# Hybrid attention block on one core: the first stage takes raw x, the norm's weight goes into the weights and its token scale into the results

## The chip, the core and the metric

The kernel runs on one core of a Trainium2 chip. The metric is the device time of one execution in microseconds (us). An execution is also profiled: its span runs from the first to the last instruction. The engines are TensorE (PE; its weight loads, PEld, stand apart), VectorE (DVE), ScalarE (ACT), GpSimd (POOL) and SyncE (SP), which issues most of the DMAs. TensorE's clock has two levels, 1.2 and 2.4 GHz, and the profile tells which was granted.

## What is computed

One decoder block over 512 tokens of width 1024, in float32. Cut to what the change touches:

```python
h = rmsnorm(x, norm_mix)          # x * rsqrt(mean(x*x) + EPS) * norm_mix
P = h @ w_in                      # q, k, v of mixer A; q, k, v (three branches) and gates of mixer B; merge gates
y_A = sliding_window_attention(...) @ w_up_a
y_B = native_sparse_attention(...) @ w_up_b
x = x + (sigmoid(g_a) * y_A + sigmoid(g_b) * y_B) @ w_out
x = x + conv_ffn(rmsnorm(x, norm_ffn))
out = rmsnorm(x, norm_final)
```

With r(t) the scale of token t, h[t, d] = x[t, d] * r(t) * norm_mix[d]. So h @ W equals r(t) times x @ (norm_mix[d] * W).

## The kernel before

A product is made of three matmuls on rounded parts (type fp32r): an operand is split into a high part (a copy that rounds) and a low part (the operand less its high part), and `three` (L104) adds high x high, high x low and low x high in PSUM. `split` (L87) makes the parts: ACT copies the high part, VectorE subtracts for the low part (L94), or GpSimd does so in pieces of 256 columns for the names in `POOLJ`.

The first stage is written out by hand. `FIRST` (L33) is a list of steps, and `do` (L178) emits each; the order of the list is the order on each engine, since engines run their queues in order. x has four tiles of 128 tokens (`t`), and the width two halves of four blocks (`h`, `k`). The steps:
- `dum`: filler matmuls on a tile of ones (L170).
- `gh`, `gl`, `ga`: high and low part of the norm weight as one row, and a matmul with ones that spreads it over the partitions (L189).
- `sq`, `ms`, `r`: squares of a tile on ACT with their sum (L195), mean on VectorE (L198, L199), power -1/2 on GpSimd (L201).
- `sc`: x times scale times norm weight, on VectorE in place (L204).
- `tp`, `xh`, `xl`: four transposes (L209), the high part `xTh` (ACT, L215) and the low part `xTl` (VectorE, L217).
- `wh`, `wl`: parts of the value weight `wv` (1024 x 408: the value columns and the branch gates), two blocks of 408 columns at a time (ACT L219, GpSimd L221).
- `v`: value matmuls (L228), 24 for each tile; a step's digits are tile, half, which of the three products, block pair.
- `va`, `la`, `vb`, `lb`, `eg`, `g`: parts of the values and the branch gates out of PSUM (L231 to L245).
- `pg`, `pgc`: the bias table spread by a one-hot matmul (L247 copies the table, L250, L253).

After it come jobs in the order `AORD` (L23): projections `ka`, `qa0`, `qa1`, `kc`, `qa2` and so on. `proj_job` (L287) loads a weight block of 1024 columns (`weight`, L96, DMA on SP), splits it, and runs 24 matmuls into a PSUM bank; its `evac` then copies the result into its slot, for `ka` `keys` (L404, ACT L413 and L414, VectorE L415 and L416), for queries `queries` (L419). PSUM has eight banks; projections use the two of tag `mm` in turn (`BANKS`, L42). `filler` (L300) feeds jobs to TensorE between the steps of the attention units; outside the first stage a planner with a simulated timeline orders the instructions. `need` (L324) asks for `ka`, `qa0` and `qa1` ahead of the first attention unit. `toeplitz` (L514) loads the bias table, stored to DRAM before, with shifted rows, into the slot that a value weight part leaves; the scores add it (L540).

Of the kernel before, what the change touches and what calls it, by code (L numbers as in the profile page):

```python
# [11 lines left out]
P = 128  # L12
# [46 lines left out]
def hybrid(tc, x, wv, wblk, w1, w2, wua, wub, wout, wfi, wfo, nmix, nffn, nfin, sinks, par, table, onehot, out):  # L59
# [9 lines left out]
    with es:  # L69
# [51 lines left out]
        wvr = [slot(7 + h, [P, 4, NV], F32, f"wvr{h}") for h in range(2)]  # L121
# [37 lines left out]
        junk = WR.tile([P, D], F32, tag="raw", name="junk", bufs=RAW)  # L159
        first = FIRST.split()  # L160
        st, ps_v, tp_x, out_v = {}, {}, {}, {}
        pgs = ((0, ZA, 0), (ZA, ZA + 512, 1), (ZA + 512, ZA + ZW, 1))

        def wv_of(w, h, c):
            return w[h][:, 2 * c : 2 * c + 2]

        def busy(n):

            for i in range(n):
                T.matmul(bank("mm", "idle"), one[:, :P], one, start=True, stop=True)  # L170
# [6 lines left out]

        def do(u):  # L178
            n = [int(c) for c in u if c.isdigit()]
            what = u.rstrip("0123456789")  # L180
            if what == "dum":
                busy((7, 2, 3, 3)[n[0] - 1])
            elif what == "gh":
                V.tensor_copy(gr[:, 0, halves[n[0]]], grow[:, halves[n[0]]])
            elif what == "gl":
                V.tensor_tensor(gr[:, 1, halves[n[0]]], grow[:, halves[n[0]]], f(gr[:, 0, halves[n[0]]]), op=ALU.subtract)
            elif what == "ga":
                for i in range(2):
                    T.matmul(gam[n[0]], one[:1, :P], gr[:, i, halves[n[0]]], start=(i == 0), stop=(i == 1))  # L189
            elif what in ("sq", "sqa", "sqb"):  # L190
                t = n[0]
                if t not in st:
                    st[t] = [SM.tile([P, c], F32, tag=g, bufs=3, name=f"{g}x_{t}") for g, c in (("s2", 2), ("ssq", 1), ("rstd", 1))]
                for i in {"sq": (0, 1), "sqa": (0,), "sqb": (1,)}[what]:
                    A.activation(junk[:, halves[i]], xt[t][:, halves[i]], AF.Square, accum_out=st[t][0][:, i : i + 1])  # L195
            elif what == "ms":
                s2, m, _ = st[n[0]]
                V.tensor_scalar(m, s2[:, 0:1], 1.0 / D, EPS, op0=ALU.mult, op1=ALU.add)  # L198
                V.tensor_scalar(m, s2[:, 1:2], 1.0 / D, m, op0=ALU.mult, op1=ALU.add)  # L199
            elif what == "r":  # L200
                G.tensor_tensor(st[n[0]][2], st[n[0]][1], mhalf, op=ALU.pow)  # L201
            elif what == "sc":
                t, h = n
                V.scalar_tensor_tensor(xt[t][:, halves[h]], xt[t][:, halves[h]], st[t][2], gam[h], op0=ALU.mult, op1=ALU.mult)  # L204
# [5 lines left out]
            elif what in ("xh", "xl"):  # L210
                t, h = n
                pv = tp_x[t, h].rearrange("p (k q) -> p k q", k=4)
                hi, lo = xTh[h][:, :, t * P : (t + 1) * P], xTl[h][:, :, t * P : (t + 1) * P]
                if what == "xh":
                    xlast[0] = A.copy(hi, pv)  # L215
                else:
                    xlast[1] = V.tensor_tensor(lo, pv, f(hi), op=ALU.subtract)  # L217
            elif what == "wh":
                A.copy(wv_of(wvh, *n), wv_of(wvr, *n))  # L219
            elif what == "wl":  # L220
                G.tensor_tensor(wv_of(wvl, *n), wv_of(wvr, *n), f(wv_of(wvh, *n)), op=ALU.subtract)  # L221
            elif what == "v":
                t, h, i, c = n
                if t not in ps_v:
                    ps_v[t] = bank(("mm", "mm", "o", "mm")[t], f"v{t}")
                mine = [w for w in first if w[0] == "v" and w[1] == str(t)]
                for k in range(4 * h + 2 * c, 4 * h + 2 * c + 2):
                    T.matmul(ps_v[t][:, :NV], (xh, xh, xl)[i](k)[:, t * P : (t + 1) * P], (wvh, wvl, wvh)[i][h][:, k % 4],  # L228
                             start=(u == mine[0] and k % 2 == 0), stop=(u == mine[-1] and k % 2 == 1))
            elif what == "va":  # L230
                A.copy(VA[:, n[0], :, 0:64], out_of(n[0])[0])  # L231
            elif what == "la":
                V.tensor_tensor(VA[:, n[0], :, 64:128], out_of(n[0])[0], f(VA[:, n[0], :, 0:64]), op=ALU.subtract)
            elif what == "vb":
                A.copy(VB[:, n[0], :, 0:64], out_of(n[0])[1])
            elif what == "lb":
                V.tensor_tensor(VB[:, n[0], :, 64:128], out_of(n[0])[1], f(VB[:, n[0], :, 0:64]), op=ALU.subtract)
            elif what == "eg":
                A.activation(out_of(n[0])[2], ps_v[n[0]][:, 384:408], AF.Exp, scale=-1.0)
            elif what == "g":  # L240
                t, eg = n[0], out_of(n[0])[2]
# [4 lines left out]
            elif what == "pg":
                V.tensor_copy(tabc, tab.rearrange("p (b h) -> p b h", b=2)[:, :, None].to_broadcast([33, 2, 16, 8]))  # L247
                for i, (c0, c1, b) in enumerate(pgs):
                    pgs_t.append(bank("pt", f"pg{c0}"))
                    T.matmul(pgs_t[i][:, : c1 - c0], tabc[:, b].rearrange("p c h -> p (c h)"), oh[:, c0:c1], start=True, stop=True)  # L250
            elif what == "pgc":
                for i, (c0, c1, b) in enumerate(pgs):
                    A.copy(gsb[:, c0:c1], pgs_t[i][:, : c1 - c0])  # L253
            else:
# [4 lines left out]
        with tc.manual_schedule():
# [5 lines left out]
            nc.scalar.dma_start(grow, nmix)  # L265
            A.activation(warm[:, 0:1], warm[:, 0:1], AF.Exp)
            for h in range(2):
                nc.sync.dma_start(xt[0][:, halves[h]], x[0:P, halves[h]])
            for h in range(2):
                for c in range(2):  # L270
                    nc.sync.dma_start(wv_of(wvr, h, c), wv[h][:, 2 * c : 2 * c + 2])
                if h == 0:
                    nc.sync.dma_start(xt[1], x[P : 2 * P])
            for t in range(2, NT):
                nc.sync.dma_start(xt[t], x[t * P : (t + 1) * P])
            nc.sync.dma_start(tab[:32], table)
            nc.sync.dma_start(oh, onehot)
            nc.sync.dma_start(prm, par)
            nc.sync.dma_start(nsink, bc(sinks, 8))
            gam = [bank("sc", f"gam{h}") for h in range(2)]  # L280
# [19 lines left out]
        def filler():  # L300
            with tc.issue_after(xlast[0].ins), tc.issue_after(xlast[1].ins):
# [158 lines left out]
        for nm in AORD.split():  # L460
# [503 lines left out]
```

## Time and profile before

| | us |
|---|---|
| median of 3 runs | 763.36 |
| lowest, highest | 761.96, 763.41 |
| profiled execution, device time | 764.42 |
| its span, first to last instruction | 762.6 |

The profiled execution is one more run of the kernel; times read from its trace are counted from the start of its span. "Busy" of TensorE counts pipelined matmuls, so that it can be near 100% at half clock too.

### The profile page before, as it was taken

How to read it: one execution, taken by the hardware profiler on the slowest of the kernel's cores; microseconds unless marked ns; L12 is line 12 of the kernel's file. 1: busy time of each engine (PE TensorE's matmuls, PEld its weight loads, DVE VectorE, ACT ScalarE, POOL GpSimd, SP SyncE). 2: the span in 40 equal slices, each digit the busy share in tenths (PEclk: the TensorE clock that was granted, in tenths of full speed). 3: DMA queues.
4: the chain of work that ended last, by engine and by line, in shares of the span. 5: the costliest groups of instructions: out<-in, count | busy, mean ns of one | idle time of the engine just before them, and what ended most of it. 6: DMA issues, size and time to landing. Idle time of an engine off the chain costs nothing.

```text
span 762.6 us, 9931 instructions
## 1 busy us (share of the span) xinstructions
PE 744.4 (98%) x3602; PEld 623.1 (82%) x3602; DVE 427.6 (56%) x902; ACT 368.2 (48%) x686; POOL 183.5 (24%) x258
## 2 busy tenths in 40 slices
PE   8999999999999999999999999999999999999996
PEld 6887787788888888878889888888888888888885
DVE  6627787456655568757365656565656564214223
ACT  6435777556656765664335444444344433113213
POOL 5234747434433545405400000000000000002001
PEclk9999999999999999999999999999999999999998
DMA  8363239312111121405322232323232324332302
GB/s 301 110 147 98 92 91 246 101 66 83 46 68 56 58 81 35 159 4 191 111 83 83 83 111 83 110 84 111 83 111 84 110 83 138 91 103 89 105 28 110
DMA packets 25582, 76.74 MB, mean 101 GB/s; under 512 B 3868, under 2 KB 6044, under 8 KB 25534
## 3 DMA queue, kind: packets, MB, share of 16 engines
q1 hardware_dynamic: 25532, 76.12, 31.3%
q8 instruction: 28, 0.46, 0.3%
q14 instruction: 20, 0.16, 0.1%
q10 hardware_dynamic: 2, 0.00, 0.0%
HBM read 72.96 MB, written 3.15 MB: 100 GB/s over the span
## 4 chain that ended last, share of the span: by engine, by line
PE 87%; DVE 5%; ACT 3%; DMA 2%; issue 2%; POOL 0%; SPq 0%; POOLq 0%; DVEq 0%; ACTq 0%
PE ug L105 11%; PE ug L106 11%; PE ug L107 10%; PE fo L857 5%; PE fo L859 5%; PE fo L858 5%; PE pT L547 2%; PE up L105 2%; PE p_ga L105 2%; PE p_ga L106 2%; PE p_ga L107 2%; PE up L107 2%; PE up L106 2%; PE wo L107 2%; PE wo L106 2%; PE wo L105 2%
## 5 line engine op out<-in xcount | busy, mean ns | idle before, releaser
L106 PE MATMUL ug<-hTl,hl_fi 128*128 128x512 f32 (+1 forms) x376 | 141.1, 375 | 0.0
L107 PE MATMUL ug<-hTh,hl_fi 128*128 128x512 f32 (+1 forms) x376 | 141.1, 375 | 0.0
L105 PE MATMUL ug<-hTh,hl_fi 128*128 128x512 f32 (+1 forms) x376 | 140.9, 376 | 0.0
L107 PEld LDWEIGHTS ug<-hTh,hl_fi 128*128 128x128 f32 x376 | 70.8, 188 | 12.9
L105 PEld LDWEIGHTS ug<-hTh,hl_fi 128*128 128x128 f32 x376 | 70.6, 188 | 12.9
L106 PEld LDWEIGHTS ug<-hTl,hl_fi 128*128 128x128 f32 x376 | 70.8, 188 | 12.6
L840 ACT ACTIVATE cv<-ug,prm 128x512 f32<-128x512 f32 x44 | 34.4, 781 | 96.2 <-PE ug L107 96.2
L883 POOL TENSOR_TENSOR X<-X,nfin 128x512 f32<-128x512 f32 x4 | 5.2, 1313 | 296.9 <-ACT junk L881 296.9
L841 DVE SCALAR_TENSOR_TENSOR cv<-ug,prm,cv 128x511 f32<-128x511 f32 x44 | 33.0, 750 | 77.0 <-ACT cv L840 76.9
L858 PE MATMUL fo<-hl_fo,AH 128*128 128x512 f32 x176 | 68.5, 389 | 0.0
L857 PE MATMUL fo<-hl_fo,AH 128*128 128x512 f32 x176 | 67.3, 389 | 0.0
L94 DVE TENSOR_TENSOR hl_fo<-raw_fo,hl_fo 128x1024 fp32r<-128x1024 f32 x22 | 27.1, 1234 | 64.6 <-ACT hl_fo L88 64.6
L88 ACT CAST hl_fo<-raw_fo 128x1024 fp32r<-128x1024 f32 x22 | 23.1, 1052 | 65.7 <-PE fo L859 65.7
L94 DVE TENSOR_TENSOR hl_fi<-raw_fi,hl_fi 128x1024 fp32r<-128x1024 f32 x44 | 53.5, 1217 | 0.8 <-ACT hl_fi L88 0.6
L859 PE MATMUL fo<-hl_fo,AL 128*128 128x512 f32 x128 | 49.8, 389 | 0.0
L477 ACT ACTIVATE Pb<-Pb,nmb 128x512 f32<-128x512 f32 (+3 forms) x64 | 35.9, 562 | 27.7 <-DVE nmb L540 26.2
L88 ACT CAST hl_fi<-raw_fi 128x1024 fp32r<-128x1024 f32 x44 | 45.6, 1039 | 1.5 <-PE wo L107 1.5
L94 DVE TENSOR_TENSOR ptl<-pT,pth 128x512 fp32r<-128x512 f32 x54 | 36.6, 685 | 15.3 <-ACT pth L88 9.9
L540 DVE CUSTOM_DVE_ANT_0 Pb<-scores,TB 128x512 f32<-128x512 f32 (+3 forms) x64 | 30.7, 486 | 16.9 <-PE scores L536 16.6
L88 ACT CAST pth<-pT 128x512 fp32r<-128x512 f32 x54 | 30.7, 584 | 19.0 <-PE pT L547 11.3
L858 PEld LDWEIGHTS fo<-hl_fo,AH 128*128 128x128 f32 x176 | 33.0, 188 | 6.9
L857 PEld LDWEIGHTS fo<-hl_fo,AH 128*128 128x128 f32 x176 | 33.0, 188 | 6.7
(317 smaller groups left out, 1729.1 us busy)
## 6 DMA issues: line engine op xcount, KB each, us to landing
raw_fi<-in_wfi_dram SPq DMA_DIRECT2D x44, 512.0 KB, 3.3
raw_fo<-in_wfo_dram SPq DMA_DIRECT2D x22, 512.0 KB, 3.3
raw_w<-in_w_dram SPq DMA_DIRECT2D x8, 512.0 KB, 3.2
raw_ga<-in_wblk_dram SPq DMA_DIRECT2D x8, 512.0 KB, 4.4
raw_gb<-in_wblk_dram SPq DMA_DIRECT2D x8, 512.0 KB, 3.3
raw_wo<-in_wout_dram SPq DMA_DIRECT2D x5, 512.0 KB, 3.5
raw_qa<-in_wblk_dram SPq DMA_DIRECT2D x4, 512.0 KB, 4.7
raw_qb<-in_wblk_dram SPq DMA_DIRECT2D x4, 512.0 KB, 3.4
```

Source lines behind the costliest of these rows:

```text
L88: A.copy(hi, src)
L94: (eng or V).tensor_tensor(lo[sl], src[sl], f(hi)[sl], op=ALU.subtract)
L105: T.matmul(ps, wh, xh, start=start, stop=False)
L106: T.matmul(ps, wh, xl, start=False, stop=False)
L107: T.matmul(ps, wl, xh, start=False, stop=stop)
L477: last_exp[0] = A.activation(a[0], a[1], AF.Exp, **k)
L540: V.tensor_tensor_reduce(ptile[:, :n], ps[:, :n], Tt[:, h, y0 : y0 + n], 1.0, HUGE, ALU.add, ALU.min, nm)
L840: A.activation(c, ps, AF.Identity, scale=cw(2, blk), bias=cb(blk))
L841: V.scalar_tensor_tensor(c[:, 1:], ps[:, : S - 1], cw(1, blk), c[:, 1:], op0=ALU.mult, op1=ALU.add)
L857: T.matmul(po[t], ah, wh, start=(k == 0), stop=False)
L858: T.matmul(po[t], ah, wl, start=False, stop=False)
L859: T.matmul(po[t], al, wh, start=False, stop=(k == NF - 1))
```

## The change

Raw x is transposed and split into `XH`, `XL`. The norm weight, transposed into a column per block (`gt`, `gc`: `gcol`), scales the value weight while it is split (`wh` on ACT, `wl` now on VectorE, one block at a time) and the weights of the first three projections (`jg` on VectorE in place, then `jh` on ACT, `jl` on GpSimd). The squares of all tiles are collected, and one mean and one power give the scale of all four tiles (`ms`, `r`). Values and gates take the scale as they leave PSUM (`va` to `eg`). A diagonal of the scale (`dg`) and a matmul with ones (`rb`, copied by `rs`) spread it along the free dimension; with it the results of `ka`, `qa0`, `qa1` are multiplied in PSUM (`m0` to `m2`). Beside that the scaled x, which all later projections read, is made: `xa` adds the two parts again on GpSimd (two pieces of 256 columns), `sc` multiplies on VectorE, `yh` and `yl` split into `xTh`, `xTl`. The three projections become steps of the list (`p`: digits are projection and block; 0 is `ka`, 1 `qa0`, 2 `qa1`), in the order 0, 2, 1. x lies in other slots, loads come in a new order, and projections `ka`, `qa0`, `qa1` are no longer jobs.

```diff
-HPJ = 24
+HPJ = 21
+LOADS = 'x00 w0 x10 w1 x20 x30 x01 w2 x11 w3 x21 x31 tab j0 prm j1 j2'
 FIRST = '''
-dum1 gh0 sqa0 gh1 gl0 sqb0 gl1 ga0 ms0 r0 ga1 wh00 sc00 dum2 wl00 sc01 wh01 tp00 tp01 xh00 dum3 wl01 sq1 xl00 v0010
...
+dum1 sq00 gt gc tp00 wh1 dum2 wh0 wl1 dum3 xh00 wl0 tp10 sq10 xl00 v0000 v0001 xh10 v0002 wh2 v1000 xl10 tp20 wh3 wl2
+v1002 sq20 v1010 wl3 v0012 xh20 v1011 sq30 v0011 xl20 v2000 v2001 sq01 v2010 tp30 wh5 v0010 wh4 wl5 v1012 xh30 wl4
+v1001 tp01 sq11 xl30 v3001 tp11 xa3 xh01 v3002 sq21 xl01 tp21 v0101 xh11 tc xa2 v0102 tp31 xh21 xl11 v1100 wh7 v1101
+xl21 xa1 xh31 v1102 wl7 v0100 sq31 pg xl31 wh6 xa0 ms jg0 v1110 pgc r v0112 wl6 v1112 xa4 v3100 dg v0111 jh0 nr v1111
+jg1 v0110 xa6 eg1 v2110 vb1 v2111 eg0 g1 vb0 rb jh1 g0 jl0 v3111 lb0 v2011 rs lb1 v2002 jg2 va1 v2100 va0 v2012 v2102
+v2112 sc3 jh2 v2101 jl1 sc0 v3012 v3011 eg2 sc2 yh0 v3101 g2 v3010 vb2 v3110 va2 la0 yh3 v3000 la2 v3102 la1 yh2 v3112
+yl3 jl2 p04 lb2 eg3 vb3 g3 p00 va3 la3 p02 lb3 sc6 p07 yl0 yh6 p01 xa7 yl2 p06 yl6 p05 xa5 sc7 p03 sc1 yh7 p22 sc4 yh1
+p20 sc5 yh4 m0 p23 yh5 yl7 p26 yl5 p24 yl1 p25 yl4 p27 p21 p11 m2 p17 p16 p14 p13 p15 p10 p12 m1'''
...
-                busy((7, 2, 3, 3)[n[0] - 1])
+                for i in range((6, 2, 3)[n[0] - 1]):
+                    T.matmul(bank("mm", "idle"), one[:, :P], one, start=True, stop=True)
...
+                T.transpose(tot[0][:, :KD], grow, ident[:KD, :KD])
+            elif what == "gc":
+                V.tensor_copy(gcol, tot[0][:, :KD])
...
+            elif what == "r":
+                G.tensor_tensor(rstd, scale, mhalf.to_broadcast([P, NT]), op=ALU.pow)
...
+            elif what == "dg":
+                V.tensor_tensor(diag.rearrange("p (t q) -> p t q", t=NT), ident[:, None, :].to_broadcast([P, NT, P]),
+                                rstd[:, :, None].to_broadcast([P, NT, P]), op=ALU.mult)
+            elif what == "rb":
+                tot.append(bank("sc", "rb"))
+                T.matmul(tot[1], f(one)[:, :P], diag, start=True, stop=True)
+            elif what == "rs":
+                A.copy(rs, tot[1])
             elif what == "wh":
-                A.copy(wv_of(wvh, *n), wv_of(wvr, *n))
+                A.mul(xu(wvh, n[0]), xu(wvr, n[0]), gcol[:, n[0] : n[0] + 1])
             elif what == "wl":
-                G.tensor_tensor(wv_of(wvl, *n), wv_of(wvr, *n), f(wv_of(wvh, *n)), op=ALU.subtract)
+                V.scalar_tensor_tensor(xu(wvl, n[0]), xu(wvr, n[0]), gcol[:, n[0] : n[0] + 1], f(xu(wvh, n[0])), op0=ALU.mult, op1=ALU.subtract)
...
+            elif what == "jg":
+                w = raws[n[0]].rearrange("p (k q) -> p k q", k=KD)
+                V.tensor_tensor(w, w, gcol[:, :, None].to_broadcast([P, KD, P]), op=ALU.mult)
+            elif what == "jh":
+                hls[n[0]] = WR.tile([P, 2, 1024], F32R, tag="hl", name=f"hl_{early[n[0]]}", bufs=3)
+                A.copy(hls[n[0]][:, 0], raws[n[0]])
+            elif what == "jl":
+                for c in range(0, 1024, 256):
+                    cs = slice(c, c + 256)
+                    G.tensor_tensor(hls[n[0]][:, 1, cs], raws[n[0]][:, cs], f(hls[n[0]])[:, 0, cs], op=ALU.subtract)
+            elif what == "p":
+                j, k = n
+                if j not in psj:
+                    psj[j] = bank(("mm", "mm", "sc")[j], f"p_{early[j]}")
+                ks = slice(k * P, (k + 1) * P)
+                three(psj[j], hls[j][:, 0, ks], hls[j][:, 1, ks], xu(XH, k), xu(XL, k), u == mine[0], u == mine[-1])
+            elif what == "m":
+                V.tensor_tensor(psj[n[0]], psj[n[0]], rs, op=ALU.mult)
+            elif what == "xa":
+                k = n[0]
+                sums[k] = AT.tile([P, S], F32, tag="P", name=f"xa{k}", bufs=8)
+                for c in range(0, S, 256):
+                    cs = slice(c, c + 256)
+                    G.tensor_tensor(sums[k][:, cs], f(xu(XH, k))[:, cs], f(xu(XL, k))[:, cs], op=ALU.add)
+            elif what == "sc":
+                V.scalar_tensor_tensor(sums[n[0]], sums[n[0]], gcol[:, n[0] : n[0] + 1], rs, op0=ALU.mult, op1=ALU.mult)
...
+                if what == "yh":
+                    last_of[0] = A.copy(xh(n[0]), sums[n[0]])
+                else:
+                    last_of[1] = V.tensor_tensor(xl(n[0]), sums[n[0]], f(xh(n[0])), op=ALU.subtract)
...
-        for nm in AORD.split():
+        done.update(early)
+        for j in range(3):
+            evacs[early[j]](psj[j])
+        for nm in AORD.split()[3:]:
```

## Rows read from the trace of the kernel before

**Rows 1.** The page: span, and the chain that ended last by engine.
```profile
span 762.6 us, 9931 instructions
...
PE 87%; DVE 5%; ACT 3%; DMA 2%; issue 2%; POOL 0%; SPq 0%; POOLq 0%; DVEq 0%; ACTq 0%
```
**Rows 2.** Windows: stretch, length, busy us (instructions) per engine, granted clock, DMA share, GB/s.
```profile
10.60:16.40 5.80, 4.92 (x29) 4.52 (x29) 4.00 (x6) 5.63 (x14) 5.54 (x5) 1.00 0.99 350
16.40:18.65 2.25, 2.18 (x6) 0.96 (x6) 2.08 (x5) 0.59 (x2) 0.68 (x3) 1.00 1.09 314
34.85:36.60 1.75, 0.00 (x0) 0.00 (x0) 1.72 (x7) 0.46 (x3) 0.82 (x1) 1.00 0.67 265
37.90:41.30 3.40, 3.40 (x9) 2.64 (x8) 0.40 (x2) 0.00 (x0) 0.00 (x0) 0.51 1.06 310
43.85:54.80 10.95, 10.93 (x49) 8.74 (x48) 4.13 (x6) 5.50 (x8) 5.65 (x8) 1.00 0.31 74
54.80:100.00 45.20, 43.05 (x235) 36.58 (x234) 33.09 (x91) 29.47 (x69) 24.82 (x36) 1.00 0.33 105
```
**Rows 3.** Timeline of TensorE: start, length, instruction (merged where equal), idle before.
```profile
1.45 3.35 PE L170 MATMUL idle<-VA 128*128 128x512 f32 x7 [1.45 <-DVE warm L262]
7.76 1.91 PE L209 MATMUL tp_x<-ident,x 128*128 128x128 f32 x8
10.67 0.61 PE L228 MATMUL v<-wvl,xTh 128*128 128x408 f32 x2
...
24.23 0.54 PEld L209 LDWEIGHTS tp_x<-ident,x 128*128 128x128 f32 x4
...
55.20 0.44 PE L105 MATMUL p_kc<-xTh,hl_kc 128*128 128x512 f32 x1
```
**Rows 4.** DMA issues to 40 us: count, KB each, median us to landing.
```profile
wvr<-in_wv_dram SPq DMA_DIRECT2D x4, 408.0 KB, 7.2
```
**Rows 5.** Groups of instructions (the last from the page): busy us, mean ns, idle before.
```profile
L228 PEld LDWEIGHTS v<-wvh,xTh 128*128 128x128 f32 x32 | 5.8, 188 | 0.0
L204 DVE SCALAR_TENSOR_TENSOR x<-x,rstdx,gam 128x512 f32<-128x512 f32 x8 | 5.8, 745 | 3.0 <-POOL rstdx L201 2.9
L217 DVE TENSOR_TENSOR xTl<-tp_x,xTh 128x512 fp32r<-128x512 f32 x8 | 5.5, 689 | 6.3 <-ACT xTh L215 6.2
L215 ACT CAST xTh<-tp_x 128x512 fp32r<-128x512 f32 x8 | 4.7, 584 | 6.5 <-PE tp_x L209 6.5
L201 POOL TENSOR_TENSOR rstdx<-ssqx,warm 128x1 f32<-128x1 f32 x4 | 2.2, 554 | 5.0 <-DVE ssqx L199 5.0
L415 DVE TENSOR_TENSOR KA<-p_ka,KA 64x512 fp32r<-64x512 f32 x2 | 1.4, 688 | 8.2 <-ACT KA L414 8.2
...
L94 DVE TENSOR_TENSOR hl_fi<-raw_fi,hl_fi 128x1024 fp32r<-128x1024 f32 x44 | 53.5, 1217 | 0.8 <-ACT hl_fi L88 0.6
```
**Rows 6.** Timelines of GpSimd and VectorE at 31, 51 and 352 us.
```profile
31.79 3.30 DVE L94 TENSOR_TENSOR hl_qa<-raw_qa,hl_qa 128x1024 fp32r<-128x1024 f32 x2 [1.21 <-ACT hl_qa L88]
32.28 3.38 POOL L94 TENSOR_TENSOR hl_ka<-raw_ka,hl_ka 128x256 fp32r<-128x256 f32 x2
...
51.09 2.83 POOL L94 TENSOR_TENSOR hl_qa<-raw_qa,hl_qa 128x256 fp32r<-128x256 f32 x4 [1.85 <-ACT hl_qa L88]
51.66 0.69 DVE L425 SCALAR_TENSOR_TENSOR QA<-p_qa,QA 64x512 fp32r<-64x512 f32 x1 [0.87 <-ACT QA L424]
...
352.04 1.22 DVE L94 TENSOR_TENSOR hl_wout<-raw_wout,hl_wout 128x1024 fp32r<-128x1024 f32 x1
352.08 4.18 POOL L94 TENSOR_TENSOR hl_wo<-raw_wo,hl_wo 128x256 fp32r<-128x256 f32 x1
354.99 0.69 DVE L779 TENSOR_TENSOR GB<-GB,GA 128x512 f32<-128x512 f32 x1
```
**Rows 7.** Timelines of GpSimd and VectorE at 12 to 16 us.
```profile
12.36 3.84 POOL L221 TENSOR_TENSOR wvl<-wvr,wvh 128x816 fp32r<-128x816 f32 x2
14.62 1.73 DVE L247 COPY gx<-gx 33x256 f32<-33x256 f32 x1 [0.18 <-DMA gx<-in_table_dram]
```

More of the change, by code (lines that the diff above doesn't have):

```diff
@@ L120, in hybrid @@
         nsink = SM.tile([P, 8], F32, tag="n8", name="nsink", bufs=1)
-        wvr = [slot(7 + h, [P, 4, NV], F32, f"wvr{h}") for h in range(2)]
+        wvr = [slot(2 + h, [P, 4, NV], F32, f"wvr{h}") for h in range(2)]
         wvh = [slot(9 + h, [P, 4, NV], F32R, f"wvh{h}") for h in range(2)]
@@ L154, in hybrid @@
         VB = slot(13, [P, NT, 4, P], F32R, "VB")
+        XH, XL = ([slot(i, [P, 4, S], F32R, f"{n}{h}") for h, i in enumerate(s)] for n, s in (("XH", (4, 5)), ("XL", (7, 8))))
+        xTh, xTl = [], []
         gate = C.tile([P, NT, 3, 8], F32, name="gate")
@@ L158, in hybrid @@
         one = VA.rearrange("p t n d -> p (t n d)")[:, :512]
-        junk = WR.tile([P, D], F32, tag="raw", name="junk", bufs=RAW)
+        junk = AT.tile([P, S], F32, tag="P", name="junk", bufs=8)
+        diag, rs = (AT.tile([P, S], F32, tag=g, name=n) for g, n in (("ptl", "diag"), ("pth", "rs")))
+        scale, rstd, nrstd, *sq2 = (SM.tile([P, NT], F32, tag=g, name=g + "x", bufs=2) for g in ("nma", "sma", "nmb", "smb", "nmc"))
         first = FIRST.split()
[L161 to L170, printed above, removed]
+        ps_v, out_v, tp_x, psj, raws, hls, sums, pgs_t, tot, last_of = {}, {}, {}, {}, {}, {}, {}, [], [], {}
+        early = AORD.split()[:3]
+        pgs = ((0, ZA, 0, 0, 0), (ZA, ZA + 512, 1, 1, 0), (ZA + 512, ZA + ZW, 1, 0, ZA))
+        xu = lambda w, k: w[k // 4][:, k % 4]
         def out_of(t):
@@ L180, in do @@
             what = u.rstrip("0123456789")
+            mine = [w for w in first if w.rstrip("0123456789") == what and w[len(what)] == str(n[0])] if n else []
             if what == "dum":
-                busy((7, 2, 3, 3)[n[0] - 1])
[L183 to L204, printed above, removed]
+                for i in range((6, 2, 3)[n[0] - 1]):
+                    T.matmul(bank("mm", "idle"), one[:, :P], one, start=True, stop=True)
+            elif what == "gt":
+                tot.append(bank("pt", "gt"))
+                T.transpose(tot[0][:, :KD], grow, ident[:KD, :KD])
+            elif what == "gc":
+                V.tensor_copy(gcol, tot[0][:, :KD])
             elif what == "tp":
@@ L212, in do @@
                 pv = tp_x[t, h].rearrange("p (k q) -> p k q", k=4)
-                hi, lo = xTh[h][:, :, t * P : (t + 1) * P], xTl[h][:, :, t * P : (t + 1) * P]
+                hi, lo = XH[h][:, :, t * P : (t + 1) * P], XL[h][:, :, t * P : (t + 1) * P]
                 if what == "xh":
-                    xlast[0] = A.copy(hi, pv)
+                    A.copy(hi, pv)
                 else:
-                    xlast[1] = V.tensor_tensor(lo, pv, f(hi), op=ALU.subtract)
+                    V.tensor_tensor(lo, pv, f(hi), op=ALU.subtract)
+            elif what == "sq":
+                t, h = n
+                A.activation(junk, xt[t][:, halves[h]], AF.Square, accum_out=sq2[h][:, t : t + 1])
+            elif what == "ms":
+                V.tensor_scalar(scale, sq2[0], 1.0 / D, EPS, op0=ALU.mult, op1=ALU.add)
+                V.scalar_tensor_tensor(scale, sq2[1], 1.0 / D, scale, op0=ALU.mult, op1=ALU.add)
+            elif what == "r":
+                G.tensor_tensor(rstd, scale, mhalf.to_broadcast([P, NT]), op=ALU.pow)
+            elif what == "nr":
+                V.tensor_scalar(nrstd, rstd, -1.0, None, op0=ALU.mult)
+            elif what == "dg":
[6 more added lines that the diff above has]
+                A.copy(rs, tot[1])
@@ L224, in do @@
                 if t not in ps_v:
-                    ps_v[t] = bank(("mm", "mm", "o", "mm")[t], f"v{t}")
-                mine = [w for w in first if w[0] == "v" and w[1] == str(t)]
+                    ps_v[t] = bank(("mm", "mm", "o", "sc")[t], f"v{t}")
                 for k in range(4 * h + 2 * c, 4 * h + 2 * c + 2):
-                    T.matmul(ps_v[t][:, :NV], (xh, xh, xl)[i](k)[:, t * P : (t + 1) * P], (wvh, wvl, wvh)[i][h][:, k % 4],
+                    T.matmul(ps_v[t][:, :NV], xu((XH, XH, XL)[i], k)[:, t * P : (t + 1) * P], xu((wvh, wvl, wvh)[i], k),
@@ L229, in do @@
                              start=(u == mine[0] and k % 2 == 0), stop=(u == mine[-1] and k % 2 == 1))
[L230 to L237, printed above, removed]
+            elif what in ("va", "la"):
+                values(VA, n[0], out_of(n[0])[0], what == "va")
+            elif what in ("vb", "lb"):
+                values(VB, n[0], out_of(n[0])[1], what == "vb")
@@ L245, in do @@
                     V.tensor_scalar(gate[:, 0, 0], gate[:, 0, 0], valid0, None, op0=ALU.mult)
+            elif what == "tc":
+                V.tensor_copy(tabc, tab.rearrange("p (b h) -> p b h", b=2)[:, :, None].to_broadcast([33, 2, 16, 8]))
             elif what == "pg":
[L247 to L250, printed above, removed]
+                pgs_t.extend(bank("pt", f"pg{i}") for i in range(2))
+                for c0, c1, b, i, d0 in pgs:
+                    T.matmul(pgs_t[i][:, d0 : d0 + c1 - c0], tabc[:, b].rearrange("p c h -> p (c h)"), oh[:, c0:c1], start=True, stop=True)
@@ L251, in do @@
             elif what == "pgc":
-                for i, (c0, c1, b) in enumerate(pgs):
-                    A.copy(gsb[:, c0:c1], pgs_t[i][:, : c1 - c0])
+                for c0, c1, b, i, d0 in pgs:
+                    A.copy(gsb[:, c0:c1], pgs_t[i][:, d0 : d0 + c1 - c0])
+            elif what == "jg":
[24 more added lines that the diff above has]
+                V.scalar_tensor_tensor(sums[n[0]], sums[n[0]], gcol[:, n[0] : n[0] + 1], rs, op0=ALU.mult, op1=ALU.mult)
+            elif what in ("yh", "yl"):
+                if not xTh:
+                    xTh.extend(slot(h, [P, 4, S], F32R, f"xTh{h}") for h in range(2))
+                    xTl.extend(slot(2 + h, [P, 4, S], F32R, f"xTl{h}") for h in range(2))
+                if what == "yh":
+                    last_of[0] = A.copy(xh(n[0]), sums[n[0]])
+                else:
+                    last_of[1] = V.tensor_tensor(xl(n[0]), sums[n[0]], f(xh(n[0])), op=ALU.subtract)
@@ L264, in hybrid @@
             G.memset(tab, 1.0)
-            nc.scalar.dma_start(grow, nmix)
+            nc.scalar.dma_start(grow, nmix.rearrange("o (k q) -> (o k) q", k=KD))
             A.activation(warm[:, 0:1], warm[:, 0:1], AF.Exp)
[L267 to L280, printed above, removed]
+            for u in LOADS.split():
+                i = int(u[-1]) if u[-1].isdigit() else 0
+                if u[0] == "x":
+                    t = int(u[1])
+                    nc.sync.dma_start(xt[t][:, halves[i]], x[t * P : (t + 1) * P, halves[i]])
+                elif u[0] == "w":
+                    c = 2 * (i % 2)
+                    nc.sync.dma_start(wvr[i // 2][:, c : c + 2], wv[i // 2][:, c : c + 2])
+                elif u == "prm":
+                    nc.sync.dma_start(prm, par)
+                    nc.sync.dma_start(nsink, bc(sinks, 8))
+                elif u == "tab":
+                    nc.sync.dma_start(tab[:32], table)
+                    nc.sync.dma_start(oh, onehot)
+                else:
+                    raws[i] = WR.tile([P, 1024], F32, tag="raw", name=f"raw_{early[i]}", bufs=RAW)
+                    nc.sync.dma_start(raws[i], wblk[BLK[early[i]][0]])
             for u in first:
@@ L300, in filler @@
         def filler():
[L301 removed]
+            with tc.issue_after(last_of[0].ins), tc.issue_after(last_of[1].ins):
                 i, nxt = 0, jobs[0][1]()
```

29 lines of the change are left out of this document (12 added, 17 removed).

## The prediction

> **What bounds the kernel now.** The page comes first: the chain that ended last is 87% TensorE, of a span of 762.6 us [rows 1], so a change pays by the TensorE time that it removes, busy or idle. Next the stretches of the first stage [rows 2]; their columns show where TensorE stands still and at which granted clock. In 10.60 to 16.40 it is idle 0.88 us, the wait for the table's copy (L247, 14.62 to 16.35 [rows 7]). In 34.85 to 36.60 it does nothing, and from 37.90 to 41.30 it works at a granted clock of 0.51, half of 2.4 GHz: 8 weight loads, so 8 matmuls of some 0.43 us, where full speed takes 10.95 / 48 = 0.228 us each [rows 2]: 1.6 us more. The timeline [rows 3] gives the marks: fillers and transposes only until 10.67, the first value matmul; `kc` from 55.20, two short score pairs ahead of it, so that the third projection leaves TensorE at 55.0. From 54.80 to 100 TensorE is busy 43.05 of 45.20 us [rows 2], so what the first stage gains or loses mostly arrives at the end.
>
> **TensorE after the change.** The value matmuls no longer wait for squares, power and scaling; they wait for a transpose of raw x and two scaled weight blocks. TensorE's queue in front of them: six fillers from 1.45, the small transpose of the norm weight, four transposes, five fillers, four transposes. Seven fillers took 3.35 us, some 0.43 each, and eight transposes 1.91 [rows 3]: 1.45 + 11 x 0.43 + 1.91 = 8.1. The first weight block is issued second instead of third, at about 1.2; the issues show 7.2 us to landing in the median [rows 4], of which the transfers ahead are a part, so I take 5.8 and 7.0; two scalings and a copy, each at most the 0.58 of a 512-wide copy [rows 5], make 8.5. Bounds 8.1 and 10.67 (where it stands now); I take 8.5. To the end of the third projection: 96 value matmuls at the 0.188 us of their weight load [rows 5], 18.0; six groups of four transposes at 0.54 [rows 3], 3.2; the table's matmuls 2.2 for 1024 columns [rows 2]; the new broadcast `rb`, 512 columns of the same type, half of that, 1.1; half clock until 10.6 as now, 1.05; 72 projection matmuls at 0.228, 16.4. That is 41.95 us from 8.5: 50.45, against 55.0. **If nothing else held TensorE back, 4.6 us would be gained**: 2.2 less 1.05 at the start, 0.9 at the table, 1.75 and 1.6 at the gap, less 1.1 for `rb`, and 0.3 in small waits. ACT has eight squares, eight `xh`, eight `wh`, three `jh`, eight `yh` and the outputs of v, some 29 us by its rows in a stretch of 46; I cost it at nothing, since TensorE's queue covers it, and a late copy costs 0.58 [rows 5] where that cover is gone.
>
> **GpSimd and VectorE: what is late next.** GpSimd gets eight sums of two pieces (`xa`) and three low parts of four pieces (`jl`) in place of four low parts of the value weight and one of a projection. Four pieces in a row take 2.83 us [rows 6], 0.71 each: 28 pieces are 19.9, and with the power (0.55 [rows 5]) 20.4. VectorE gets the low parts of the value weight, three `jg` (1024 columns, 1.22 [rows 5]), `dg`, eight `sc` and eight `yl`, and loses the scaling of x (8 x 0.75 [rows 5]) and two low parts. What the two do to each other stands in [rows 6]. Beside two VectorE low parts two pieces took 3.38 us, and those two VectorE instructions 3.30 where 1.22 each is usual. One piece took 4.18 us: for 3.6 us of it VectorE ran five instructions without a break, the first a low part, the last an add (L779), all with both inputs in SBUF. Four pieces beside a `queries` instruction, which reads PSUM, took the plain 2.83. So VectorE work with both inputs in SBUF, low part or not, nearly adds up with GpSimd's: in the first case 1.96 us of GpSimd lost to 2.44 us of VectorE work (0.8 per us), in the second 3.47 to 3.6 (0.96).
>
> One more instruction could count. The table's copy (`tc`) has one input, and two pieces of 816 columns took 3.84 us with it beside the second [rows 7], 1.92 each: not slowed. The Trainium skill, GPSIMD Engine Reference, 8. Key points, says that GpSimd contends with VectorE instructions that have two SBUF inputs and with those in a 2-port mode; the trace agrees on the first, 1.69 against 0.71. If `tc` ran in that mode, the rule would put up to 1.4 us on the sums below and 0.8 on the time; the row says none, and I go by the row.
>
> Now the walk. The transposes of tile 3's first half are behind 24 value matmuls: 8.5 + 4.5 + two groups 1.1 + half clock 1.05 = 15.1; copy and low part (0.58, 0.69 [rows 5]) end at 16.5, and the sums start there. Alone GpSimd would end its list at 36.9. Before its last sum VectorE has two low parts of the value weight (0.6 each), three `jg` (3.7), `dg` (0.6), six `sc` at 0.6 to 0.75 and four `yl` at 0.6: 11.5 us with both inputs in SBUF. At 0.8 GpSimd loses 9.2, and **the last sum ends at 46.1** (bounds 36.9 and 47.9). `sc5` (0.75) and `m0` (0.69, as L217), queued behind it, make 47.6: the first projection's result is scaled 8 us after its last matmul. The evacuation of `ka` (ACT 0.58, four VectorE parts of 0.69 [rows 5]) and four `yl` follow, 6.1 us: 53.7. `kc` needs the bank that `ka` leaves and can't start sooner; now it starts at 55.20. `jl2` ends some 4.4 us ahead of the last sum, 41.7, while the projection that reads it starts at 39.55 and asks for it piece by piece: waits of about 1 us, so the third projection ends at 51.4. TensorE is then idle 2.3 us. After the old gap of 1.75 us its clock stood at half for 3.4 us; at the 0.88 us it did not fall [rows 2]. So what follows the gap costs 0 to 1.6 us; I take half, 0.8. Sum: `kc` begins 1.5 us earlier, less 0.8: 0.7 us gained.
>
> **The rest.** SP issues x in halves and three projection weights earlier; at the 350 GB/s of 10.60 to 16.40 [rows 2] all 5.4 MB are there by about 19 us, ten and more before the projections read them: nothing. The table's store and the toeplitz loads wait for the value weight's slot as now, hidden behind `kc`; without that cover the first scores would come 1 to 4 us late. The queries' evacuation now follows all projections, some 3.5 us of VectorE beside `kc` (24 x 0.228 = 5.5): nothing, as long as `kc` runs. The profiled execution took 764.42 us, its span and 1.8 around it: 764.42 - 0.7 = 763.7. The median of the runs lies 1.06 lower: **762.7 us**.
>
> **The rivals.**
> 1. The shared work costs little, and TensorE's own sum decides. For it: VectorE's new work comes with waits between, in which pieces get through at 0.71. Then `kc` starts at 50.5 to 51.5 behind a gap under 1 us: 4 us gained, 759.3 (758.4 to 760.4). Against it: every piece beside such work in [rows 6] was slowed.
> 2. Slower: GpSimd starves as in the 4.18 us piece wherever `jg`, `sc` and `yl` follow each other. With 0.96, and with 5 us of later `sc` and `yl` also ahead of the sums, GpSimd loses 15.8: the last sum ends at 52.7, `jl2` at 46. The projection that reads it waits 5 us, half clock behind it (1.6), and `kc` starts near 58, 2.8 us late, part of that at half clock again: 766.0 (765 to 768). It decides from a mean piece of about 1.2 us. Against it: in the first case of [rows 6] the two took turns.
> 3. The start comes no earlier: the first weight block lands at the median 7.2 us after its issue or later [rows 4], the value matmuls begin near 10.6 as now, and sums and `kc` shift by 2 us: 764.8 (764 to 765.5).
>
> **How the numbers follow.** About 0.2%, 1.5 us, is what a measurement of this kernel can tell from no change: faster is under 761.8, slower above 764.9. Forecast 0.42; its own range is 761.4 to 764.2 (half clock or not, last sum between 44 and 47), 0.06 of it faster. Rival 1 has 0.30, faster. Rival 2 has 0.20, slower. Rival 3 has 0.08, half of it slower; the forecast's upper tail adds 0.03. Faster 0.36, same 0.37, slower 0.27. The range, 759.2 to 766.2, takes in more than half of rivals 1 and 2 each and leaves out some 0.1 on either side.
>
> **What would show it.** Right: value matmuls from about 8.5; GpSimd pieces of 0.9 to 1.2 us in the mean; the last sum near 46; `m0` behind `sc5`; an idle TensorE of 2 to 3 us ahead of `kc`, which starts near 54. Rival 1 shows pieces of 0.75 to 0.85 and hardly a gap at `kc`; rival 2 single pieces of 3 us and more, and a gap inside the second projection computed (`qa1`); rival 3 a first value matmul after 10. The prediction is wrong where the start is right and the gap at `kc` is missing, or where the stages after 100 us move by over 2 us by themselves.

## The result, and the profile after

The changed kernel takes 759.58 us in the median of 5 runs (758.53 to 760.13), the kernel before 763.36 on the same chip (761.96 to 765.57): a ratio of 0.9943, 95% interval 0.9924 to 0.9961. It is 3.8 us faster, more than a measurement's uncertainty. The forecast was 762.7 with a range from 759.2, so the time lies inside the range near its lower end, but the gain is five times the 0.7 us of the sum, and no change was taken to be the likeliest outcome. The profiled execution took 759.33 us, its span is 757.5, 5.1 us under that of before; the two profiled executions lie on opposite sides of their medians, which makes 1.3 us of that.

TensorE in the first stage, after (start, length, instruction, idle before), to be held against [rows 3]:

```profile
1.45 2.92 PE L191 MATMUL idle<-VA 128*128 128x512 f32 x6 [1.45 <-DVE warm L301]
4.31 0.27 PE L194 MATMUL gt<-ident,gx 8*128 8x8 f32 x1
4.51 1.11 PE L201 MATMUL tp_x<-ident,x 128*128 128x128 f32 x4
5.28 2.11 PE L191 MATMUL idle<-VA 128*128 128x512 f32 x5
7.23 0.60 PE L201 MATMUL tp_x<-ident,x 128*128 128x128 f32 x4
7.58 0.62 PE L237 MATMUL v<-wvh,XH 128*128 128x408 f32 x2
8.04 0.53 PE L237 MATMUL v<-wvl,XH 128*128 128x408 f32 x2
8.41 0.53 PE L237 MATMUL v<-wvh,XL 128*128 128x408 f32 x2
...
30.44 0.91 PE L237 MATMUL v<-wvh,XL 128*128 128x408 f32 x4
34.13 0.76 PE L110 MATMUL p_ka<-XH,hl_ka 128*128 128x512 f32 x1 [2.79 <-ACT xTh L291]
...
52.05 0.39 PE L110 MATMUL p_kc<-xTh,hl_kc 128*128 128x512 f32 x1
```

Values begin at 7.58 instead of 10.67, and at full speed: the next pair starts 0.46 us later, the one after 0.37. Ahead of `ka` TensorE stands still 2.79 us. `kc` follows the third projection with no gap, at 52.05 instead of 55.20. The windows (columns as in [rows 2]) show the price of the gap, and the attention stages behind:

```profile
31.30:34.10 2.80, 0.04 (x1) 0.00 (x0) 2.77 (x6) 2.34 (x6) 2.80 (x4) 0.97 0.43 171
34.10:37.40 3.30, 3.27 (x8) 2.62 (x9) 3.27 (x11) 0.74 (x3) 3.30 (x6) 0.51 0.64 206
52.05:97.30 45.25, 44.09 (x240) 37.75 (x239) 36.68 (x96) 33.02 (x73) 25.80 (x41) 1.00 0.33 115
```

In the gap VectorE and GpSimd are both busy throughout; behind it the clock is at half for 3.3 us, as behind the old gap. From `kc` on TensorE is idle 1.16 us in 45.25; before it was idle 2.15 in 45.20 [rows 2]. Of the 5.1 us between the two spans, 3.15 are there when `kc` starts, and 1.95 come later. What GpSimd and VectorE do meanwhile (timelines, equal instructions merged):

```profile
9.26 1.06 POOL L283 TENSOR_TENSOR xa<-XH,XL 128x256 f32<-128x256 f32 x1 [7.37 <-DVE XL L209]
14.62 5.30 POOL L283 TENSOR_TENSOR xa<-XH,XL 128x256 f32<-128x256 f32 x7 [4.30 <-DVE XL L209]
20.02 1.95 POOL L217 TENSOR_TENSOR smax<-nmax,warm 128x4 f32<-128x4 f32 x1
...
26.22 3.81 POOL L269 TENSOR_TENSOR hl_ka<-raw_ka,hl_ka 128x256 fp32r<-128x256 f32 x4
29.99 7.36 POOL L269 TENSOR_TENSOR hl_qa<-raw_qa,hl_qa 128x256 fp32r<-128x256 f32 x8
37.31 4.62 POOL L283 TENSOR_TENSOR xa<-XH,XL 128x256 f32<-128x256 f32 x4
```

```profile
29.36 3.50 DVE L285 SCALAR_TENSOR_TENSOR xa<-xa,gx,rs 128x512 f32<-128x512 f32 x3
...
33.73 0.77 DVE L183 SCALAR_TENSOR_TENSOR VA<-v,smax,VA 128x128 fp32r<-128x128 f32 x3
...
44.39 0.69 DVE L277 TENSOR_TENSOR p_ka<-p_ka,rs 128x512 f32<-128x512 f32 x1
...
50.72 0.69 DVE L458 TENSOR_TENSOR KA<-p_ka,KA 64x512 fp32r<-64x512 f32 x1
```

The low part of `ka`'s weight is ready at 30.0, so `ka` does not wait for it. The profile puts the gap down to an ACT copy (`xTh`), which `ka` neither reads nor needs; that name only marks what ended last. The bank of tag `mm` that `ka` gets held the values of tile 0. Its last reader is `la0`, the first of the three `VA` low parts at 33.73, queued on VectorE behind three `sc` that took 3.50 us together, 1.17 each. The scaling of before, which has one input in PSUM, takes 0.75 [rows 5]. That reading is tested first.

### The profile page after: what moved, and what is told of

Its sections match the earlier page's. It is cut to its first block, busy times and chain, and to the rows that moved or that the text cites. A ratio compares the mean times of both kernels' runs of the same rounds, so it can differ in the third digit from the quotient of the medians.

```text
span 757.5 us, 9971 instructions
## 1 busy us (share of the span) xinstructions
PE 741.2 (98%) x3600; PEld 621.3 (82%) x3600; DVE 447.5 (59%) x915; ACT 375.6 (50%) x699; POOL 198.1 (26%) x275
## 3 DMA queue, kind: packets, MB, share of 16 engines
HBM read 72.96 MB, written 3.15 MB: 100 GB/s over the span
## 4 chain that ended last, share of the span: by engine, by line
PE 86%; DVE 5%; ACT 4%; issue 2%; POOL 1%; DMA 1%; SPq 0%; POOLq 0%; ACTq 0%; DVEq 0%
PE ug L112 11%; PE ug L110 11%; PE ug L111 11%; PE fo L902 5%; PE fo L904 5%; PE fo L903 5%; PE pT L592 2%; PE up L110 2%; PE p_ga L111 2%; PE p_ga L110 2%; PE up L112 2%; PE p_ga L112 2%; PE up L111 2%; PE wo L112 2%; PE wo L110 2%; PE wo L111 2%
```

## The experiments

All ratios are to the kernel before, timed in the same session; the medians of before in the four sessions lie between 763.4 and 764.5, so ratios are compared, not medians.

### The bank, and the two inputs

**e1_bank.**

```diff
-                    psj[j] = bank(("mm", "mm", "sc")[j], f"p_{early[j]}")
+                    psj[j] = bank(("pt", "mm", "sc")[j], f"p_{early[j]}")
```

> The changed kernel, with the first projection (ka) in a PSUM bank of the transposes (tag pt) instead of the bank that the values of tile 0 leave. Theory (bank): the 2.79 us that TensorE stands still at 31.3 us is the wait for that bank, whose last reader (la0 on VectorE) is queued behind three sc that took 3.50 us; so ka starts near 31.3, there is no half clock behind it, the third projection ends near 47.8 instead of 52.05, and kc starts between 48 and 49.5, when its own low parts (now 46.2 to 50.2) and the last yl (47.5) are there: 756.0 to 757.5. Rival (weights): ka waits for something that it reads, the low part on GpSimd or what ACT does at 34 us; then the gap stays at 2.5 to 3 us and the time at 759 to 760.5.

756.71 us, ratio 0.9902 (0.9884 to 0.9921). Order and engines are as in the changed kernel. TensorE in `e1_bank`, around `ka` and `kc`, and VectorE's last part of `ka`:

```profile
30.30 0.73 PE L237 MATMUL v<-wvh,XL 128*128 128x408 f32 x3
30.86 0.39 PE L110 MATMUL p_ka<-XH,hl_ka 128*128 128x512 f32 x1
...
47.23 0.39 PE L110 MATMUL p_kc<-xTh,hl_kc 128*128 128x512 f32 x1
...
53.40 0.30 PE L580 MATMUL scores<-KA,QA 128*128 128x130 f32 x1 [0.21 <-DVE QA L467]
...
54.66 0.33 PE L580 MATMUL scores<-KA,QA 128*128 128x130 f32 x1 [0.85 <-DVE QA L467]
```

```profile
50.49 0.69 DVE L458 TENSOR_TENSOR KA<-p_ka,KA 64x512 fp32r<-64x512 f32 x1
```

No gap, no half clock: `ka`'s wait was for the bank. The edit does a second thing. The banks of tag `mm` are handed out in turn, so with `ka` gone from them `kc` no longer gets the bank that `ka` leaves: it starts at 47.23, while the last part of `ka` is read until 51.18. `kc` comes 4.8 us earlier than in the changed kernel, by both of these and by the half clock that is missing; the run does not part them. The end comes only 2.5 us earlier: 1.06 us go into two waits of the first scores for the queries, whose evacuation hangs on VectorE, and the rest was not traced.

**e2_scpsum.**

```diff
-                V.scalar_tensor_tensor(sums[n[0]], sums[n[0]], gcol[:, n[0] : n[0] + 1], rs, op0=ALU.mult, op1=ALU.mult)
+                V.scalar_tensor_tensor(sums[n[0]], sums[n[0]], gcol[:, n[0] : n[0] + 1], tot[1], op0=ALU.mult, op1=ALU.mult)
```

> The changed kernel, with the eight sc reading the spread scale from the PSUM bank of rb instead of its copy in SBUF, so that they have one input in SBUF, not two; nothing else moves. Theory (shared access): GpSimd and a VectorE instruction exclude each other only where both its inputs lie in SBUF; so an sc takes about 0.75 us instead of 1.17 beside GpSimd, GpSimd's 28 pieces fall from 0.95 us in the mean to 0.80 to 0.88, la0 comes 1.3 us or more earlier, the gap ahead of ka shrinks to 1 to 1.5 us and with it perhaps the half clock: 756.5 to 758.5. Rival (sc is slow by itself, from its column scale or its length): an sc stays at 1.1 to 1.2, the gap at 2.5 to 3, the time at 759 to 760.5.

755.99 us, ratio 0.9895 (0.9877 to 0.9913), a little below the range expected. VectorE, GpSimd and TensorE in `e2_scpsum`:

```profile
29.17 2.05 DVE L285 SCALAR_TENSOR_TENSOR xa<-xa,gx,rb 128x512 f32<-128x512 f32 x3
29.80 6.08 POOL L269 TENSOR_TENSOR hl_qa<-raw_qa,hl_qa 128x256 fp32r<-128x256 f32 x8
31.96 0.47 PE L110 MATMUL p_ka<-XH,hl_ka 128*128 128x512 f32 x1 [0.82 <-ACT VA L181]
```

The same three instructions, at the same place, take 2.05 us instead of 3.50, GpSimd's eight pieces beside them 6.08 instead of 7.36, and the gap is 0.82 instead of 2.79. One input in SBUF or two is what decides here, beside GpSimd. GpSimd's mean over all 28 pieces falls only from 0.95 to 0.88, the end of what was expected, probably because other VectorE work beside it still has two inputs in SBUF; that was not tried.

**e7_no_xa.** The eight steps `xa`, 16 pieces on GpSimd, are taken out of the list `FIRST`, so the scaled x lacks the low part of x, and `sc` reads the high part:

```diff
             elif what == "sc":
-                V.scalar_tensor_tensor(sums[n[0]], sums[n[0]], gcol[:, n[0] : n[0] + 1], rs, op0=ALU.mult, op1=ALU.mult)
+                sums[n[0]] = AT.tile([P, S], F32, tag="P", name=f"xa{n[0]}", bufs=8)
+                V.scalar_tensor_tensor(sums[n[0]], f(xu(XH, n[0])), gcol[:, n[0] : n[0] + 1], rs, op0=ALU.mult, op1=ALU.mult)
```

> The changed kernel without the sixteen pieces of xa: sc reads the high part of x in place of the sum, so the scaled x lacks the low part of x. Theory (shared access): GpSimd has 12 us less and its first three low parts come 6 us earlier; three sc take 2.1 to 2.6 us, la0 comes early, the gap ahead of ka is under 1 us, and kc starts near 48: 755.0 to 757.0. Rival: the gap comes from VectorE's own queue (jg, sc and the gates, some 12 us by their plain lengths between 22 and 34), whatever GpSimd does: gap 2 us or more, 758.5 to 760.

756.37 us, ratio 0.9894 (0.9869 to 0.9919), as expected, but the instructions did not do what was expected:

```profile
26.14 8.38 POOL L269 TENSOR_TENSOR hl_qa<-raw_qa,hl_qa 128x256 fp32r<-128x256 f32 x8
27.88 3.52 DVE L286 SCALAR_TENSOR_TENSOR xa<-XH,gx,rs 128x512 f32<-128x512 f32 x3
32.68 0.47 PE L110 MATMUL p_ka<-XH,hl_ka 128*128 128x512 f32 x1 [1.14 <-ACT xTh L292]
...
38.00 2.73 DVE L286 SCALAR_TENSOR_TENSOR xa<-XH,gx,rs 128x512 f32<-128x512 f32 x4
```

The three `sc` still take 3.52 us, since GpSimd does low parts of the weights beside them here too; everything merely starts 1.5 us earlier. The four `sc` at 38.00 also have both inputs in SBUF, but GpSimd does nothing from 34.66 to 40.84, and they take 0.68 us each, no more than those of e2 with one input in PSUM. So it is the two SBUF inputs and GpSimd's work together that make 1.17. Taking 16 of GpSimd's 28 pieces away gains no more than one operand moved to PSUM.

**e5_both**, the edits of e1 and e2 together:

> The changed kernel with both edits: ka in a bank of tag pt, and sc reading the scale from PSUM. Theory: no gap ahead of ka, three sc in 2.05 us, the third projection ends near 47.3, m0 near 41.5; then the first scores (53.4 in e1_bank, which waited for the queries' low parts on VectorE) come at 50 to 51.5, since VectorE has 2 us less to do: 754.3 to 755.6. Rival: with the gap gone, the queries' evacuation behind the third projection sets the scores anyway, and both edits together give no more than one of them: 755.7 to 757.

755.45 us, ratio 0.9883 (0.9862 to 0.9905): the lowest of all, 8.7 us under its own session's before, though its interval overlaps those of e1 and e2. No gap ahead of `ka` (31.62) or `kc` (47.99), but the first scores came at 53.43, not at 50 to 51.5: they stand behind `kc`'s 24 matmuls in TensorE's queue. The time lies in the first range expected, though the step that was to bring it did not come. So the two edits add little to each other.

### The start

**e4_late.**

```diff
-                for i in range((6, 2, 3)[n[0] - 1]):
+                for i in range((6, 2, 17)[n[0] - 1]):
```

> The changed kernel, with 14 more fillers ahead of the second tile's transposes, so that the first value matmul comes about 3 us later, near where it was before the change (10.67). Theory (start): the value stage, the sums and all behind them hang on that start, and nothing takes it up: plus 2.5 to 3 us, 762.0 to 762.8. Rival (the sums and low parts on GpSimd and VectorE set the pace behind 20 us, and the weights that they need come from the DMAs): the later start is partly taken up by the gap of 2.79 us ahead of ka, which shrinks: plus 0.5 to 1.5 us, 760.0 to 761.2.

763.22 us, ratio 0.999 (0.9977 to 1.0002): the whole gain is gone. The first sum starts at 12.57 instead of 9.26, 3.3 us later, and the time rises by 3.6, a little more than expected. Nothing takes the start up, since the sums hang on it too. TensorE in `e4_late`:

```profile
37.44 0.47 PE L110 MATMUL p_ka<-XH,hl_ka 128*128 128x512 f32 x1 [2.78 <-ACT xTh L291]
...
54.92 0.47 PE L110 MATMUL p_kc<-xTh,hl_kc 128*128 128x512 f32 x1 [0.88 <-DVE KA L458]
```

**e8_loads.**

```diff
-LOADS = 'x00 w0 x10 w1 x20 x30 x01 w2 x11 w3 x21 x31 tab j0 prm j1 j2'
+LOADS = 'x00 x01 w0 w1 x10 x11 w2 w3 x20 x21 x30 x31 tab j0 prm j1 j2'
```

> The changed kernel with the loads near the order of before: both halves of tile 0 of x first, then two weight blocks, then both halves of tile 1, and so on. If the early start rests on the new order of the loads as much as on raw x, the transposes of tile 1 and 2 wait for their halves, the first value matmul comes at 8 to 9 us, the stage ends 1 to 2 us later: 760.8 to 762. If raw x alone makes it, the loads have room: under 0.5 us, 759.2 to 760.3.

762.97 us, ratio 0.9982 (0.9971 to 0.9993), worse than either expectation. TensorE and ACT in `e8_loads`, and the ACT row of the changed kernel that answers to it:

```profile
7.01 1.16 ACT L229 ACTIVATE wvh<-wvr,gx 128x408 fp32r<-128x408 f32 x2 [2.87 <-DMA wvr<-in_wv_dram]
8.62 0.66 PE L201 MATMUL tp_x<-ident,x 128*128 128x128 f32 x4 [1.23 <-DMA x<-in_x_dram]
...
12.29 0.66 PE L201 MATMUL tp_x<-ident,x 128*128 128x128 f32 x4 [1.51 <-DMA x<-in_x_dram]
```

```profile
5.00 1.16 ACT L229 ACTIVATE wvh<-wvr,gx 128x408 fp32r<-128x408 f32 x2 [0.88 <-DMA wvr<-in_wv_dram]
```

With the old sort of order the first weight block is there at 7.01, 2 us later, and two groups of transposes wait 2.7 us for x. So the start is bought by raw x and the order of the loads together; with the old sort of order about a third of the gain is left, by the ratios.

### The old gap by itself

**e3_old_pool.** The kernel before, with `qa0 qa1` added to `POOLJ`.

> The kernel before the change, with the low parts of qa0 and qa1 on GpSimd instead of VectorE, nothing else. Theory (queue): the old gap of 1.75 us and the half clock behind it came from the outputs of the values queued on VectorE behind those two low parts; so the gap goes, and this alone gives 2.5 to 3.5 us: 760.0 to 761.0. If so, most of what the change gains could be had without raw x. Rival: the gap moves to the next wait, since GpSimd has three low parts in a row (8.5 us from 31 us on) and the first projections wait for them, or the planner orders the rest in another way: 762.5 to 764.5.

760.83 us, ratio 0.9956 (0.9938 to 0.9975). TensorE in this kernel is 1.75 us busy of 1.75 in the old place of the gap (last window):

```profile
14.88:15.83 0.95, 0.00 (x1) 0.00 (x1) 0.95 (x2) 0.95 (x3) 0.75 (x1) 1.00 1.01 392
18.00:21.30 3.30, 3.30 (x11) 3.14 (x10) 2.51 (x6) 0.72 (x2) 0.68 (x2) 0.51 0.83 337
34.85:36.60 1.75, 1.75 (x11) 1.57 (x10) 1.72 (x6) 0.62 (x3) 1.75 (x3) 1.00 0.44 101
```

That one line gives 2.9 us, and its interval overlaps that of the whole change. The values of before were held up by VectorE's queue in the same way as `la0` is now. The other two windows belong to the clock: the wait at the table took 0.95 us here, and 2.2 us after it the clock stood at half for 3.3 us, though in the kernel before, behind 0.88 us at the same step [rows 2], it is 1.00 from 16.40 to 34.85.

### The clock behind the gap

**e0_again**, the changed kernel, and **e6_old_again**, the kernel before, once more:

> The changed kernel once more, beside the others on the same chip. 758.5 to 760.5. If the half clock behind the gap ahead of ka is a matter of when the gap falls, this profile can lack it as e4_late lacked it (2.78 us idle, clock at full), and the third projection then ends 1.5 us earlier; if it follows from the gap's length, it is there again.

> The kernel before the change once more, for a second profile. The gap of 1.75 us ahead of ka should be there; the half clock behind it and the rise of the clock at 10.6 us may come at other times, as in e3_old_pool, where value matmuls started at 9.27. kc between 53.5 and 55.5; 762 to 765.5.

`e0_again`: 759.94 us, ratio 0.9937 (0.9919 to 0.9956). `e6_old_again`: one run, 763.3; the gap is there with 1.84 us, half clock behind it, and its first two pairs of value matmuls, from 10.74, still run at half speed (0.94 and 0.88 us, against 0.62 and 0.53 above), although the granted clock of 10.70 to 12.20 is given as 1.00. `e0_again` around its gap, windows and TensorE:

```profile
31.00:34.00 3.00, 0.57 (x3) 0.51 (x4) 2.97 (x8) 2.94 (x8) 3.00 (x4) 1.00 0.31 127
34.00:37.50 3.50, 3.50 (x17) 2.88 (x16) 3.46 (x10) 0.31 (x2) 3.50 (x5) 1.00 0.92 227
```

```profile
33.43 0.47 PE L110 MATMUL p_ka<-XH,hl_ka 128*128 128x512 f32 x1 [2.79 <-ACT xTh L291]
...
50.91 0.47 PE L110 MATMUL p_kc<-xTh,hl_kc 128*128 128x512 f32 x1 [0.88 <-DVE KA L458]
```

The gap is the same to 0.01 us and the clock stays at full. So the half clock does not follow from the gap's length alone. Without it the third projection ends earlier, and then `kc` waits 0.88 us for the last `KA` part: the bank that `ka` leaves.

**e9_fill.** Eleven fillers through the gap, named `dum4` in the list of the order, behind `v3112`:

```diff
-                for i in range((6, 2, 3)[n[0] - 1]):
-                    T.matmul(bank("mm", "idle"), one[:, :P], one, start=True, stop=True)
+                for i in range((6, 2, 3, 11)[n[0] - 1]):
+                    src = xu(XH, 0) if n[0] == 4 else one
+                    T.matmul(bank("pt" if n[0] == 4 else "mm", "idle"), src[:, :P], src, start=True, stop=True)
```

> The changed kernel with 11 filler matmuls (some 2.4 us at full clock) between the last value matmul and ka, into a bank of the transposes, so that TensorE works through the gap of 2.79 us. The gap itself stays, ka starts near 33.4 to 34.1 as before; what goes is the half clock behind it in the executions that have it. Theory: that half clock costs 1.5 us where it comes, of which kc's wait for the bank of ka (0.88 us in e0_again) takes up more than half, so the median gains 0.2 to 0.8: 758.8 to 759.6, with less spread. Rival: the half clock is worth the full 1.5 us in most executions: 758.0 to 758.6.

759.29 us, ratio 0.9933 (0.9918 to 0.9947). Full clock through the gap, `kc` again 0.89 us behind `ka`'s bank. The ratio differs from that of the changed kernel by less than either interval, and the spread is no smaller (758.28 to 760.42), so this run doesn't settle how much the half clock is worth; its median speaks against the full 1.5 us of the rival's range.

## Why the prediction was wrong

**The bound on `kc`** is the step that carried the forecast, and it failed: the evacuation of `ka`, behind the last sum on GpSimd, was to hold `kc` until 53.7, and half clock behind that wait was to cost another 0.8. The evacuation ended at 51.41 (50.72 + 0.69), and in the changed kernel's first profile it held nothing: TensorE itself reached `kc` at 52.05. In `e0_again` it did hold `kc`, but only until 50.76. The terms behind this, one by one:

**The start.** I took 8.5 us for the first value matmul; it came at 7.58, and at 6.83 in `e0_again`. One step that was off is the landing of the first weight block: issued at 1.17 it was in use at 5.00, 3.8 us, where I had taken 5.8. I had taken that from transfers that stood behind two others, although the new order leaves only one ahead. So TensorE's own queue sets the start, with no wait from 4.31 on, and that is 0.5 us shorter than my 8.1, mainly because the second group of transposes took 0.35 us (7.23 to 7.58), at full speed, where I had taken half of 1.91. The "half clock until 10.6", 1.05 us, was read from lengths alone: in the kernel before, the granted clock of 5.00 to 10.60 is given as 1.00, while its fillers take twice the time of a matmul at full speed.

```profile
5.00:10.60 5.60, 5.60 (x17) 3.93 (x17) 2.48 (x5) 3.57 (x9) 3.26 (x3) 1.00 1.00 386
```

In the changed kernel's profiles the value matmuls run at full speed from the first one on; that slow stretch is no fixed part of the kernel's start. The earlier start and this stretch make 2.0 us together. `e4_late` shows that this start is worth its full length, and `e8_loads` that the load order, which I costed at nothing beyond the first block, carries it. How much of the 3.1 us between the two first profiles is the change's own stays open: in `e3_old_pool`, which has the old start, the first value matmul came at 9.27, and eight transposes ahead of it took 1.31 us instead of 1.91.

**The table's wait** went as said, and so, roughly, did the size of TensorE's own work: 23.8 us from the first value matmul to the last, against 25.6 in the sum (18.0 + 3.2 + 2.2 + 1.1 + 1.05; the terms for the table and `rb` were too much, and the half clock's). The cause of the old gap went too, but a longer gap came in its place.

**GpSimd against VectorE** was right as a mechanism and measured in e2 and e7: pieces of 0.95 us in the mean in the changed kernel, within the 0.9 to 1.2 of the forecast. Its sum was mis-sized: the last sum ended at 41.9, not 46.1. Of the 4.2 us, 1.9 come from the start (the sums ran from 14.62, not 16.5), 0.7 from a first piece at 9.26, which needs only the tiles 0 and 1, and which I had missed; the loss was 7.6 us, not 9.2. Part of it sits in an instruction I had counted at 0.55, the length for one column: the power on four columns took 1.95 (20.02 to 21.97), and no run parts what the columns and what VectorE's work beside it add. From the last sum to the end of `ka`'s evacuation it took 9.5 us, not 7.6, since `m0` stood behind four `sc` (3.21 us from 41.26) and not `sc5` alone; so 2.3 of the 4.2 us arrive there.

**The gap** came in the wrong place. I put 2.3 us ahead of `kc`, where `m0` and the evacuation of `ka` would hold the bank; the step was right in kind and small, 0.88 us where no half clock hides it. I missed the same wait one projection earlier: nothing in the prediction asks whether the bank that `ka` writes is free, and its last reader stood behind three `sc` on VectorE, 2.79 us. The 1 us that I gave to the second projection's weights did not come.

**After `kc`** I passed the gain on unchanged. The attention stages gave 1.95 us more (1.3 between `e0_again` and `e6_old_again`: 756.5 - 50.91 against 761.5 - 54.65). Waits of before, such as 1.70 us at `kw` and 1.21 at `ksl`, are gone or down to 0.2 in the new order of the planner; the waits of the scores grew from 0.3 to 1.0 us. That this stems from the new order of `kc` and the scores is argued, not tried.

The measured time is that of rival 1, 759.3, yet rival 1 was not what happened: its pieces of 0.75 to 0.85 are absent and a gap is there. The start gave what the gap took, so the time's place inside the range is luck. Rivals 2 and 3 did not come.

## What to carry to other kernels

When a stage is moved forward, check for each first matmul both what it reads and who still reads the bank that it writes, and follow that reader's queue on its engine. Where GpSimd and VectorE work side by side, count VectorE's instructions with both inputs in SBUF; moving one operand to PSUM can be worth as much as taking more than half of GpSimd's pieces away (16 of 28). Time a load from its place in the queue, and before rewriting a stage, look for the instructions ahead of the gap that could go to another engine: one line gave some three quarters of this change's gain.

## What the runs showed of the hardware that was not expected

A gap of 2.79 us left TensorE's granted clock at half for 3.3 us in one execution and at full in another of the same kernel. In `e3_old_pool` half clock came after a gap of only 0.95 us. VectorE pays for the sharing as GpSimd does: an instruction of 512 columns with both inputs in SBUF took 1.17 us beside GpSimd and 0.68 where GpSimd stood idle. The Trainium skill, GPSIMD Engine Reference, 8. Key points, names contention of GpSimd with VectorE instructions that have two SBUF inputs. The runs agree: with one input moved to PSUM the VectorE instructions lost their delay beside GpSimd (2.05 us for three against 3.50).
